# A mixture-of-experts encoder on one core: five token tiles gathered, five multiplied densely, expert blocks summed four at a time

## The chip, the cores and the metric

The kernel runs on one core of a Trainium2 chip. The metric is device time in microseconds, median of the runs; lower is better. One execution was taken by the hardware profiler, and every row below comes from it.

## What is computed

An encoder layer for 1280 tokens (256 of a prompt, 1024 of a sample) of width 1024, in fp32: a mixer (retention and latent attention), cross attention to 256 memory tokens, and a layer of experts, cut here to what matters:

```python
q = (xt @ wq).reshape(128, 8, 256)
s1, s2 = q1 . sub_keys[0], q2 . sub_keys[1]      # 8 heads, 128 keys each
v1, i1 = top_k(s1, 16); v2, i2 = top_k(s2, 16)
ts, sel = top_k(v1[:, None] + v2[None, :], 16)   # ids = i1 * 128 + i2: 16 experts of 16384 per head
g = softmax(ts)
a = einsum('td,ted->te', xt, U[ids])             # 128 experts a token
y = einsum('te,ted->td', g * gelu(a), V[ids])
```

U and V have 16384 rows of 1024 floats. A last RMS norm follows.

## The kernel before, in words

The tokens are ten tiles of 128. After the mixer and cross attention (lines 307 to 870) the experts of a tile are computed in one of two ways, and the list GATHER (line 39) says which.

**Routing** (`lists`, `pairs`, `route`, lines 879 to 992) finds a tile's 128 experts a token with VectorE's top-8 instructions. A tile in GATHER then stores its ids; a dense tile stores the two key numbers and the weight. The last dense tile (KEPT, line 44) hands them over in SBUF instead, and the first dense tile of the last block (HALVED) is routed in two halves.

**Gathered tiles** (`gather`, line 995): for each of 128 expert slots GpSimd issues an indirect DMA that fetches one row of U per token (128 rows of 4 KB, line 1025), and VectorE multiplies it with the tokens and sums (line 1031); 128 slots of V follow, each scaled and added to an accumulator (line 1040). That is 256 row steps a tile. In the pass tokens and accumulator lie in PSUM. Nine row buffers take turns there (line 119 has four, `gather` adds two, and three come at line 147 when the routing is done and its room is given back).

**Dense tiles**: first `gates` (line 1067) makes a table G of every token's weight for every expert from one-hot products, tile by tile, with VectorE, ScalarE, GpSimd and TensorE at work; a step that needs an unrouted tile runs the routing until it is there (line 1082). Then `dense` (line 1147), the **dense pass**, walks the 128 blocks of 128 experts. `a_stage` loads a block of U and V, splits each into a high and a low part (ScalarE copies, GpSimd subtracts: uh, ul, vh, vl), multiplies U with the tokens of both halves of the dense tiles in three matmuls per chunk of 128 (lines 173 to 175), applies Gelu (ScalarE), the gate (VectorE, wr) and splits the result (wh by ScalarE, wl by VectorE). `v_stage` multiplies with V for each tile and sums NG blocks in PSUM before VectorE adds the sum to the tile's accumulator (line 1212). NG is 3: 43 groups. A group's second product is written behind the next group's first one.

**What sets the order of the work.** The program is one Python trace; the tile framework may move instructions by its own view of time, and each engine then runs its own in order. Routing and gathering are generators. After each group of three matmuls `mm3` (line 176) calls `tick` with an estimate of TensorE's time, `tick` (line 123) multiplies it by a share from RHO (line 50; the third pair is the dense pass: first number while tiles are being routed, second while rows alone are left) and `step` (line 136) takes steps from the generators until their own estimates (1.2 for a row, 0.65 to 2.6 for pieces of routing) have used it up. `step` takes routing first and gathering when no routing is left. What is left when the pass has been written comes behind it (line 1268). VectorE's instructions of routing and of rows go through `Fill` (line 80), which ties each behind the last instruction of the main work written before it (`Lead`, line 64): the framework may let it fall later, not draw it ahead of that. For the steps left behind the pass that mark is the pass's start (line 1267).

```python
q = q or self.routing or self.gathering          # line 137
self.slots, self.at = ["grow"] * 4, 0            # line 119
wl = ap.tile([P, H], F32R, tag="wl", ..., bufs=2 * NG + 3)   # line 1185; vh, vl: 2 * NG + 1
```

SyncE's queue issues the loads of U, V and G and the small loads at the start of a gathered tile (ids, weights, tokens, lines 1012 to 1018); GpSimd's queue issues the row fetches, between its subtractions.

## Time and profile before

| | us |
|---|---|
| median of 3 runs | 4372.47 (4365.78 to 4373.7) |
| the profiled execution | 4367.04 |
| its span, first to last instruction | 4365.2 |
| first dense matmul in the profile | 2111.45 |

The engines are PE (TensorE), PEld (its weight loads, which overlap PE), DVE (VectorE), ACT (ScalarE), POOL (GpSimd) and SP (SyncE, DMA issue); a q behind a name is its sequencer. Times are us, and L with a number is a line of the kernel. In a row of the windows each engine has its busy time and instructions; the granted share of TensorE's clock, the mean busy share of 16 DMA engines and what they moved follow. In a row of groups the mean of one instruction is in ns, and behind the second bar stands the engine's idle time just before them with what ended it. Matmuls overlap each other, so the time of one is longer than the distance of two starts. L74 stands for all instructions through `Lead`, L90 for those through `Fill`.

### The profile page before, as it was taken

The page shows a single profiled execution, that of the slowest core. Times are in us where ns is not written, and L with a number is a line of the kernel's source. Part 1 is how long each engine was busy: PE and PEld are TensorE (multiplying, and loading weights), DVE is VectorE, ACT ScalarE, POOL GpSimd, SP SyncE. Part 2 cuts the span into 40 slices and gives each one's busy share as a digit, 9 for nine tenths or more (in the row PEclk, how much of TensorE's full clock was granted, in tenths as well). Part 3 has the DMA queues.
Part 4 walks back from the last instruction along what each step waited for, and adds up shares of the span by engine and source line. Part 5 has one row for each costly group of instructions (what it writes and reads, how often), then busy time and mean ns, then how long its engine had stood idle before and what let it go on. Part 6 is the DMA issues. An engine that isn't in the chain of part 4 may idle for free.

```text
span 4365.2 us, 66436 instructions
## 1 busy us (share of the span) xinstructions
PE 4010.5 (92%) x23202; PEld 3578.9 (82%) x23202; DVE 3281.7 (75%) x7044; ACT 1639.9 (38%) x3569; POOL 2301.6 (53%) x2090
## 2 busy tenths in 40 slices
PE   7999988899788988887798999999999999999999
PEld 7999877666587877876787888888988889888888
DVE  5556422798576799699788878888887888878883
ACT  6333535455343243498522222222222223222223
POOL 2221244013667710277537776666777677766662
PEclk9999999899899989999999999999999999999999
DMA  2112578237789866577648988888888889888882
GB/s 89 37 40 71 202 240 286 80 103 223 261 271 334 278 227 228 186 219 211 212 127 295 325 302 297 311 294 299 310 307 301 285 300 328 316 298 295 289 286 85
DMA packets 489008, 1030.74 MB, mean 236 GB/s; under 512 B 42720, under 2 KB 201952, under 8 KB 488672
## 3 DMA queue, kind: packets, MB, share of 16 engines
q0 software_dynamic: 149536, 545.33, 35.5%
q1 hardware_dynamic: 329200, 470.66, 32.6%
q10 hardware_dynamic: 9936, 10.51, 0.8%
q8 instruction: 182, 2.98, 0.3%
q14 instruction: 154, 1.26, 0.1%
HBM read 901.87 MB, written 124.45 MB: 235 GB/s over the span
## 4 chain that ended last, share of the span: by engine, by line
PE 26%; issue 8%; POOL 6%; DVE 6%; DMA 3%; ACT 1%; SPq 0%; POOLq 0%; ACTq 0%; DVEq 0%
PE pa L175 5%; PE pa L173 5%; PE pa L174 5%; PE pv L174 4%; PE pv L173 4%; PE pv L175 4%; POOL grow L1025 4%; DMA ur<-in_uT 2%; POOL vl L1199 1%; POOL ul L1175 1%; DVE gps L90 1%; DVE wr L74 1%; DVE dacc L74 1%; DVE wl L74 1%; DVE gj L90 1%
## 5 line engine op out<-in xcount | busy, mean ns | idle before, releaser
L1025 POOL DMA_INDIRECT grow<-in_peer_u,gids x512 | 537.1, 1049 | 533.9 <-DVE gj L90 213.0
L1025 POOL DMA_INDIRECT grow<-in_peer_v,gids x512 | 522.5, 1020 | 545.5 <-DVE gps L90 159.9
L173 PE MATMUL pa<-dxT,uh 128*128 128x384 f32 x2048 | 689.0, 337 | 17.4 <-ACT wr L1186 15.0
L174 PE MATMUL pa<-dxT,uh 128*128 128x384 f32 x2048 | 688.6, 336 | 0.0
L175 PE MATMUL pa<-dxT,ul 128*128 128x384 f32 x2048 | 676.4, 337 | 9.3 <-POOL ul L1175 9.3
L173 PE MATMUL pv<-vh,wh 128*128 128x512 f32 x1536 | 603.7, 397 | 40.1 <-DVE dacc L74 40.1
L174 PE MATMUL pv<-vl,wh 128*128 128x512 f32 x1536 | 609.7, 397 | 12.4 <-POOL vl L1199 11.7
L175 PE MATMUL pv<-vh,wl 128*128 128x512 f32 x1536 | 608.9, 396 | 1.4 <-DVE wl L74 1.4
L90 DVE SCALAR_TENSOR_TENSOR gps<-grow,ga,gps 128x1024 f32<-128x1024 f32 x384 | 493.2, 1284 | 9.6 <-ACT gps L1052 2.9
L90 DVE SCALAR_TENSOR_TENSOR gj<-grow,gps 128x1024 bf16<-128x1024 f32 x384 | 466.7, 1215 | 11.2 <-DMA grow<-in_peer_u,gids 3.1
L206 POOL TENSOR_TENSOR wl<-wraw,wh 128x512 fp32r<-128x512 f32 x180 | 250.7, 1409 | 310.7 <-ACT wh L202 241.2
L173 PEld LDWEIGHTS pa<-dxT,uh 128*128 128x128 f32 x2048 | 386.4, 189 | 31.7 <-ACT wr L1186 16.5
L1199 POOL TENSOR_TENSOR vl<-vr,vh 128x512 fp32r<-128x512 f32 x256 | 331.2, 1313 | 146.4 <-ACT vh L1198 144.3
L175 PEld LDWEIGHTS pa<-dxT,ul 128*128 128x128 f32 x2048 | 385.2, 189 | 21.2 <-POOL ul L1175 15.6
L1175 POOL TENSOR_TENSOR ul<-ur,uh 128x512 fp32r<-128x512 f32 x256 | 337.3, 1321 | 106.8 <-ACT uh L1174 103.5
L74 DVE TENSOR_TENSOR dacc<-pv,dacc 128x1024 f32<-128x1024 f32 x258 | 311.8, 1218 | 108.1 <-PE pv L175 107.6
L174 PEld LDWEIGHTS pa<-dxT,uh 128*128 128x128 f32 x2048 | 386.3, 189 | 6.3
L173 PEld LDWEIGHTS pv<-vh,wh 128*128 128x128 f32 x1536 | 292.7, 191 | 104.6 <-DVE dacc L74 48.5
L1174 ACT CAST uh<-ur 128x512 fp32r<-128x512 f32 x256 | 158.3, 621 | 553.4 <-DMA ur<-in_uT 510.2
L74 DVE TENSOR_TENSOR wr<-wr,gt 128x384 f32<-128x384 f32 x256 | 196.2, 767 | 209.2 <-ACT wr L1186 184.2
L174 PEld LDWEIGHTS pv<-vl,wh 128*128 128x128 f32 x1536 | 293.2, 191 | 73.2 <-POOL vl L1199 18.4
L175 PEld LDWEIGHTS pv<-vh,wl 128*128 128x128 f32 x1536 | 292.9, 191 | 58.4 <-DVE wl L74 1.8
(287 smaller groups left out, 9373.8 us busy)
## 6 DMA issues: line engine op xcount, KB each, us to landing
ur<-in_uT SPq DMA_DIRECT2D x256, 256.0 KB, 4.1
vr<-in_peer_v SPq DMA_DIRECT2D x256, 256.0 KB, 4.0
G<-st SPq DMA_DIRECT2D x96, 512.0 KB, 6.2
gt<-G SPq DMA_DIRECT2D x64, 768.0 KB, 7.2
wraw<-in_peer_wq SPq DMA_DIRECT2D x96, 256.0 KB, 5.9
wraw<-in_w_out SPq DMA_DIRECT2D x48, 256.0 KB, 5.1
wraw<-in_ca_wq SPq DMA_DIRECT2D x48, 256.0 KB, 3.6
x<-ld SPq DMA_DIRECT2D x24, 512.0 KB, 6.6
```

Source lines behind the costliest of these rows:

```text
L74: r = f(*a, **kw)
L90: r = f(*a, **kw)
L173: mm(ps, a[0], b[0], start=first, stop=False)
L174: mm(ps, a[0], b[1], start=False, stop=False)
L175: mm(ps, a[1], b[0], start=False, stop=last)
L206: (nc.vector if self.spare and k in self.spare else eng).tensor_tensor(wl[:, :n], raw[:, :n], r32(wh[:, :n]), ALU.subtract)
L1025: nc.gpsimd.indirect_dma_start(out=u, out_offset=None, in_=src, in_offset=bass.IndirectOffsetOnAxis(ap=ids[:, s:s + 1], axis=0))
L1174: nc.scalar.copy(uh, ur)
L1175: nc.gpsimd.tensor_tensor(ul, ur, r32(uh), ALU.subtract)
L1199: nc.gpsimd.tensor_tensor(vl, vr, r32(vh), ALU.subtract)
```

## The change

Tile 7 joins GATHER, so five tiles are gathered and five (2 to 6) are dense; tile 6 is then both HALVED and KEPT. The dense tokens are split into halves of 384 and 256 columns. NG becomes 4, which makes 32 groups and gives W 11 and V 9 buffers. In the dense pass `step` takes gathering and routing in turn, and the share for rows alone is 0.78.

```diff
--- before.py
+++ after.py
@@ -36,7 +36,7 @@
 EPS, GEPS = 1e-6, 1e-5
 NDEC = RH * P + 5 * RH
 
-GATHER = [0, 1, 8, 9]
+GATHER = [0, 1, 7, 8, 9]
 DENSE = [t for t in range(NTILE) if t not in GATHER]
 TD = len(DENSE) * P
 MADE = DENSE
@@ -44,10 +44,10 @@
 HALVED, KEPT = [t for t in MADE if t in BLOCKS[-1]][0], MADE[-1]
 TG = 64
 HP = PK // 2
-NG = 3
+NG = 4
 O1_BY = "va"
 
-RHO = ((0.75, 0.7), (0.5, 0.0), (0.9, 0.55))
+RHO = ((0.75, 0.7), (0.5, 0.0), (0.9, 0.78))
 LATE = 2
 
 MORE = 3
@@ -117,6 +117,7 @@
         self.owed, self.rho = 0.0, (0.0, 0.0)
         self.gps = self.rp = None
         self.slots, self.at = ["grow"] * 4, 0
+        self.turn = 0
         self.anchor = None
         self.v, self.vf = Lead(self), Fill(self)
 
@@ -134,7 +135,12 @@
             self.owed -= self.step()
 
     def step(self, q=None):
-        q = q or self.routing or self.gathering
+        if q is None:
+            q = self.routing or self.gathering
+            if self.rho is RHO[2] and self.gathering:
+
+                self.turn += 1
+                q = (self.gathering if self.turn % 2 else self.routing) or q
         try:
             return next(q[0])
         except StopIteration:
@@ -1149,7 +1155,9 @@
         dx, xT = self.dx, self.xT
         v = self.v
         nd = len(DENSE)
-        H = TD // 2
+
+        H = nd // 2 * P + nd % 2 * P
+        halves = [(0, H), (H, TD)]
         NTG = TD // TG
         vb = I["peer_v"].rearrange("(b i) d -> b i d", b=PK)
         with ExitStack() as es:
@@ -1176,7 +1184,8 @@
                         U.append((uh, ul))
                     Wb = []
                     for hf in range(2):
-                        hs = slice(hf * H, (hf + 1) * H)
+                        c0, c1 = halves[hf]
+                        hs, H = slice(c0, c1), c1 - c0
                         ps = pa.tile([P, 512], F32, tag="pa", name=self.nm("pa"))
                         for k in range(KC):
                             self.mm3(ps[:, :H], [u[:, k % 4, :] for u in U[k // 4]], (xT[0][:, k, hs], xT[1][:, k, hs]), k == 0, k == KC - 1)
@@ -1185,7 +1194,7 @@
                         wl = ap.tile([P, H], F32R, tag="wl", name=self.nm("wl"), bufs=2 * NG + 3)
                         nc.scalar.activation(wr, ps[:, :H], AF.Gelu)
                         w3 = wr.rearrange("p (g t) -> p g t", t=TG)
-                        v.tensor_tensor(w3, w3, self.gt[:, hf * NTG // 2:(hf + 1) * NTG // 2, n % 2, :], ALU.mult)
+                        v.tensor_tensor(w3, w3, self.gt[:, c0 // TG:c1 // TG, n % 2, :], ALU.mult)
                         nc.scalar.copy(wh, wr)
                         v.tensor_tensor(wl, wr, r32(wh), ALU.subtract)
                         Wb.append((wh, wl))
@@ -1204,7 +1213,7 @@
 
             def v_stage(W, V):
                 for n in range(nd):
-                    hf, at = divmod(n * P, H)
+                    hf, at = divmod(n * P, halves[0][1])
                     ps = pv.tile([P, D], F32, tag="pv", name=self.nm("pv"))
                     for j in range(len(W)):
                         for c in range(2):
```

## Rows read from the trace of the kernel before

**Rows 1.** The page, part 1: busy us, share of the span, instructions.
```profile
PE 4010.5 (92%) x23202; PEld 3578.9 (82%) x23202; DVE 3281.7 (75%) x7044; ACT 1639.9 (38%) x3569; POOL 2301.6 (53%) x2090
```

**Rows 2.** Windows of the dense pass: length; PE, PEld, DVE, ACT, POOL; clock, DMA, GB/s.
```profile
2111.00:2272.00 161.00, 139.02 (x694) 125.27 (x693) 126.44 (x505) 49.48 (x85) 56.41 (x41) 0.96 0.50 159
2272.00:4256.00 1984.00, 1925.34 (x9566) 1734.55 (x9565) 1644.55 (x1899) 515.08 (x939) 1397.39 (x1262) 0.99 0.85 301
4256.00:4365.20 109.20, 101.16 (x502) 90.44 (x500) 42.94 (x53) 35.38 (x63) 24.14 (x19) 0.98 0.25 85
```

**Rows 3.** Waits, 2300 to 4250 us: total us, times, longest us.
```profile
POOL grow L1025 <- DVE gps L90: 180.6, 123, 10.3
...
DVE wr L74 <- ACT wr L1186: 157.9, 73, 6.6
...
PE pv L173 <- DVE dacc L74: 31.7, 13, 4.1
...
PE pv L174 <- POOL vl L1199: 11.7, 8, 3.7
```

**Rows 4.** Timeline of TensorE in the pass, 384 columns: start us, us.
```profile
2111.71 0.34 PE L174 MATMUL pa<-dxT,uh 128*128 128x384 f32 x1
...
2117.95 0.33 PE L174 MATMUL pa<-dxT,uh 128*128 128x384 f32 x1
```

**Rows 5.** Timeline of TensorE, first projections, 256 columns.
```profile
149.79 0.28 PE L175 MATMUL pj<-wh,xl 128*128 128x256 f32 x1
...
154.07 0.28 PE L175 MATMUL pj<-wh,xl 128*128 128x256 f32 x1
```

**Rows 6.** Timeline of TensorE in the pass, second product, 512 columns.
```profile
3310.08 0.39 PE L174 MATMUL pv<-vl,wh 128*128 128x512 f32 x1
...
3316.88 0.39 PE L174 MATMUL pv<-vl,wh 128*128 128x512 f32 x1
```

**Rows 7.** Windows, tile grow alone (row buffers): DVE, ACT, POOL busy; clock, DMA, GB/s.
```profile
2272.00:4256.00 1984.00, 1036.69 (x1202) 7.02 (x12) 810.56 (x808) 0.99 0.85 301
```

**Rows 8.** Groups by line, 2111 to 4366 us: busy, mean ns, idle before.
```profile
L1175 POOL TENSOR_TENSOR ul<-ur,uh 128x512 fp32r<-128x512 f32 x253 | 333.5, 1321 | 106.8 <-ACT uh L1174 103.5
L1199 POOL TENSOR_TENSOR vl<-vr,vh 128x512 fp32r<-128x512 f32 x256 | 331.2, 1313 | 146.4 <-ACT vh L1198 144.3
L74 DVE TENSOR_TENSOR dacc<-pv,dacc 128x1024 f32<-128x1024 f32 x258 | 311.8, 1218 | 108.1 <-PE pv L175 107.6
...
L74 DVE TENSOR_TENSOR wl<-wr,wh 128x384 fp32r<-128x384 f32 x256 | 231.8, 906 | 66.5 <-ACT wh L1189 64.4 <-PE pv L175 1.6
L74 DVE TENSOR_TENSOR wr<-wr,gt 128x384 f32<-128x384 f32 x256 | 196.2, 767 | 209.2 <-ACT wr L1186 184.2 <-ACT root L186 21.1 <-DMA vr<-in_peer_v 3.5
```

**Rows 9.** Timeline of GpSimd and VectorE, 3338 to 3390 us.
```profile
3338.52 0.94 POOL L1025 DMA_INDIRECT grow<-in_peer_v,gids  x1 [0.30 <-issue]
3339.77 0.94 POOL L1025 DMA_INDIRECT grow<-in_peer_v,gids  x1 [0.31 <-issue]
...
3364.02 5.03 POOL L1199 TENSOR_TENSOR vl<-vr,vh 128x512 fp32r<-128x512 f32 x4
...
3365.41 4.05 DVE L74 TENSOR_TENSOR wl<-wr,wh 128x384 fp32r<-128x384 f32 x1
...
3389.01 0.55 DVE L74 TENSOR_TENSOR wl<-wr,wh 128x384 fp32r<-128x384 f32 x1
```

**Rows 10.** A window of 20 us in the pass, columns as in rows 2.
```profile
3040.00:3060.00 20.00, 20.00 (x99) 17.64 (x98) 15.86 (x25) 4.84 (x9) 16.75 (x16) 1.00 1.02 402
```

**Rows 11.** Waits of SyncE's DMA queue, 2300 to 4250 us.
```profile
SPq L1014 <- DVE ga L90: 14.7, 1, 14.7
```

**Rows 12.** Windows of the gate making, 1827 to 2111 us, summed; timeline of TensorE there.
```profile
sum 284.00, PE 222.50 PEld 196.57 DVE 275.65 ACT 261.49 POOL 216.79; mean PE 55.62 PEld 49.14 DVE 68.91 ACT 65.37 POOL 54.20
...
2065.56 0.42 PE L1093 MATMUL ps<-c_ident,g 128*128 128x128 f32 x1
...
2111.45 0.42 PE L173 MATMUL pa<-dxT,uh 128*128 128x384 f32 x1
```

## The prediction

> **What bounds the kernel now.** I read the page's busy times first: TensorE is busy 92% of the span, VectorE 75%, GpSimd 53% [rows 1]. A mean over stages says little, so next come the windows. From 2111 us to the end (2254 us) runs the dense pass, and in its main stretch of 1984 us TensorE is busy 1925 us at a granted clock of 0.99, VectorE 1645, GpSimd 1397, the DMA engines 0.85 [rows 2]. The waits say which way the engines lean on each other [rows 3]: VectorE waits for ScalarE's Gelu (157.9 us), which waits for TensorE; GpSimd waits for VectorE to give a row buffer back (180.6 us); TensorE waits for an eviction 31.7 us in all. So TensorE bounds the pass, and the rows of the gathered tiles ride along. The pitch of its matmuls, first start against last, is 0.1733 us at 384 columns (36 in 6.24 us [rows 4]), 0.1189 at 256 (36 in 4.28 us [rows 5]) and 0.2267 at 512 (30 in 6.80 us [rows 6]). 6144 x 0.1733 + 4608 x 0.2267 = 2109 us of the 2254.
>
> **Sum made against** the profiled execution, 4367 us (span 4365.2), 5 us under the median of 4372.5.
>
> **TensorE.** Five dense tiles: the first product has 3072 matmuls of 384 and 3072 of 256 columns, 532 + 365 us; the second has 3840 of 512, 871 us. Together 1768 us, 341 less than now. Weight loads need no term of their own: the 0.1189 was measured with one load per matmul. Where TensorE waits more, its clock may fall; at the 0.96 of the pass's first stretch [rows 2] the same work takes 1842 us, still less than what follows.
>
> **VectorE.** In the pass it is busy 126 + 1645 + 43 = 1814 us [rows 2]. One more gathered tile is 256 rows; all work on row buffers took 1036.69 us for 808 rows [rows 7], 1.283 us each with the start and finish of a tile in it: +328. Evictions fall from 43 groups x 6 tiles = 258 to 32 x 5 = 160, at 1.218 us [rows 8]: -119. The gate product and the residue (wr, wl) keep their 512 instructions; a half of them get a third narrower, and of the 0.55 us that one takes undisturbed [rows 9] I let a third go: 256 x 0.18 = -46. Routing of tile 7 moves into the pass. It has no clean row: the 126 us that VectorE was busy in the first 161 us of the pass hold two tiles' routing, wr, wl and evictions, so one tile is under 63 us; 30 would leave over half of the stretch to the others. I take 45, nearer the middle, and keep 30 and 63 as ends. Sum 1814 + 328 - 119 - 46 + 45 = **2022 us**, more than TensorE's 1768. VectorE becomes the longer one.
>
> The mean wr and wl (0.767 and 0.906 us [rows 8]) lie well over 0.55, and one row shows why: a wl of 4.05 us starts inside a GpSimd run of four vl subtractions of 5.03 us and ends with it [rows 9]. I keep the excess of 256 x (0.22 + 0.36) = 148 us as it is; if each further GpSimd instruction held VectorE as much, it would grow with GpSimd's work below (a fifth), by 30 us, and that is the other end. The Trainium skill, SBUF — State Buffer, section "Who interferes with whom", says that a VectorE instruction with two SBUF inputs contends with a GpSimd one that reads SBUF, and not with one that only writes. By that rule the ul and vl subtractions count, whose number does not change; the sum would be the 2022 us, against 2052 by the other end.
>
> **GpSimd.** A row's descriptors take 810.56/808 = 1.003 us [rows 7], and from one to the next 1.25 us pass where nothing is waited for (3338.52 to 3339.77 [rows 9]). Now 812 of them stand in the pass (44 rows are left of tile 0, and three tiles), after the change 1068. With 512 subtractions at 1.32 us [rows 8] the queue needs 812 x 1.25 + 676 = 1691 us now, and 1068 x 1.25 + 676 = **2011 us** after. That is level with VectorE, and in order: a descriptor that waits for a row buffer holds the ul and vl behind it, for which TensorE waits.
>
> **DMA.** 159 x 161 + 301 x 1984 + 85 x 109 = 632 MB in the pass [rows 2]; 256 rows of 0.524 MB make 766. The best 20 us moved 402 GB/s at a share of 1.02 [rows 10]; at that rate 1905 us. SP gets four loads and a store more, for one more tile's start and end; the ids load at a tile's start held SP 14.7 us [rows 11], with weight loads queued behind it. I cost that at nothing, since four raw buffers stand ahead; without that cover it is 15 us. ScalarE is busy 600 us of the pass [rows 2] and gets copies of under 10 us more: nothing.
>
> **Where the rows stand.** The planner credits the gathering 0.78 of its own estimate of TensorE's time (line 50) and charges 1.2 for a row (lines 1032, 1041). Its estimate for the pass is 128 x 12.8 = 1638. While three tiles are routed in turn with rows (35.4 units each, 0.9 credited) 245 pass with 95 rows; the other 1393 x 0.78 / 1.2 give 906. So 1001 of 1068 rows stand in the pass, and **67 behind it**, where they may be drawn forward only behind the row before them. Before, the same count ends at 1851 of 1966, which is the idle end in the last 109 us of rows 2. Nine row buffers are there as before, but three of them only when routing is done, now about 15% into the pass.
>
> **The pass after.** VectorE's 2022, plus its waits. wl on ScalarE's copy, 66.5 us [rows 8], stays: it is a latency. The waits for TensorE, 157.9 at wr [rows 3] and 108.1 at the eviction [rows 8], shrink as TensorE gets ahead; none left would be 0, all left 266. I keep a quarter, 66 us, nearer to none, since TensorE has 1768 us of work against 2022. Start and end idled 35 + 66 us [rows 2]; rows now begin with the pass and fill its end, and I keep 30. 2022 + 66 + 66 + 30 = 2184 us, **70 less** than 2254.
>
> **Ahead of the pass.** Gate making for six tiles runs from 1827 us to the first dense matmul at 2111.45; VectorE is busy 275.65 of 284 us and ScalarE 261.49 [rows 12]. The sixth tile (7) got its last transpose at 2065.56, so its own piece is 46 us, and at least that goes. A sixth of the stage and 45 us of routing, 92, go at most. ScalarE then binds: 261.49 x 5/6 = 218, and I add some 10 for its first transposes: 228, **56 less**.
>
> Sum: 4367 - 56 - 70 = 4241.
>
> **Rivals.**
> A, the three queues dovetail: the waits for TensorE vanish and the pass ends with VectorE's 2022 and 38 us: 4117. For it: in gate making VectorE is busy 275.65 of 284 us [rows 12], 0.97, beside a ScalarE as full. Against: GpSimd's 2011.
> B, the DMA engines bind. At the main stretch's 301 GB/s for 0.85 [rows 2] full is 354: 766 MB take 2164 us, and with 70 us of thin start and end 2234: 4291. Against: the 402 of rows 10. The Trainium skill, DMA: Bandwidth & Descriptors, section "Where 436 GB/s comes from", gives about 358 GB/s as the limit between HBM and SBUF; by it 2140 us, and the sum would be 4267. The 20 us at 402 do not agree with it as a ceiling.
> C, slower: a convoy. GpSimd stands at a descriptor until VectorE frees a row buffer, the vl behind it are late, TensorE is late, and VectorE waits at wr in its own order. Then VectorE's share stays what it is, 1814/2254 = 0.805, and 2022/0.805 = 2512 us give 4569. It decides under 2022/2310 = 0.875. For it: the 180.6 us in which GpSimd stands at such descriptors, and 11.7 us of TensorE waiting for vl [rows 3]; with four blocks a group holds eight vl where it held six, and only one vl can be made ahead of a group, as now. Against: nearly all of VectorE's other idle time now is waiting for TensorE, which will be ahead.
> D, it does not do what it says: the scheduler places instructions by its own view of time, and if the pass holds no more rows than at 0.55, 95 + 1393 x 0.55/1.2 = 733, then 335 stand behind it at 1.283: 430 us after 1768 and TensorE's idle 144: 2342 us, 4399.
>
> **How the numbers follow.** Forecast 0.56, A 0.15, B 0.11, C 0.13, D 0.05. The predicted time is 4241. The range goes down to A (4117) and up past B and the forecast's bad ends (266 - 66 of waits, 30 of contention, 18 of routing: 4489 together, 4365 for half of it) to 4370; it leaves out C, D and half of A. Under 0.2% (9 us) a measurement of this kernel cannot tell from no change. Faster 0.80 (forecast, A, most of B), same 0.06, slower 0.14.
>
> **What would show it.** Right: first dense matmul near 2055 us; 256 rows more and 98 evictions fewer in the pass; VectorE at 0.92 or more and TensorE near 0.82 of the pass; GpSimd's subtractions and descriptors nearly back to back; about 67 rows after the last second product. Wrong: TensorE still above 0.93 (A), DMA share at 0.97 with rows late (B), VectorE under 0.88 with long waits of TensorE for vl (C), hundreds of rows at the end (D).

## The result, and the profile after

The changed kernel takes 4395.3 us (median of 6 runs, 4389.4 to 4405.4), the kernel before 4370.9 on the same chip: a ratio of 1.0061, with a 95% interval of 1.0048 to 1.0074. It is slower by 0.6%; 4241 was forecast, with 0.14 for slower. The profiled execution has a span of 4391.6 us against 4365.2, 26 more: gate making and what lies ahead of it give back 64 (the first dense matmul starts at 2047.3 instead of 2111.45 [rows 12]), and from there to the end it is 2344 us instead of 2254, 90 more where 70 less were forecast.

The page, part 1 (busy us, share of the span, instructions), which answers to [rows 1]:

```profile
PE 3715.7 (85%) x22175; PEld 3280.2 (75%) x22175; DVE 3393.2 (77%) x7220; ACT 1548.1 (35%) x3465; POOL 2488.2 (57%) x2314
```

The windows of the pass (length; PE, PEld, DVE, ACT, POOL busy; clock, DMA share, GB/s), cut where its routing ends and where the last second product ends; they answer to [rows 2]:

```profile
2047.30:2470.00 422.70, 370.90 (x1983) 330.24 (x1982) 385.38 (x1001) 122.78 (x229) 241.40 (x201) 0.94 0.73 239
2470.00:4219.40 1749.40, 1547.85 (x8006) 1360.36 (x8004) 1460.49 (x1873) 428.56 (x863) 1348.83 (x1262) 0.95 0.94 341
4219.40:4391.60 172.20, 0.00 (x0) 0.00 (x0) 162.69 (x130) 2.85 (x6) 108.52 (x115) 0.51 0.94 366
```

And the same windows for the tile grow alone (row buffers: DVE, ACT, POOL busy; clock, DMA share, GB/s), as in [rows 7]:

```profile
2047.30:2470.00 422.70, 140.36 (x151) 1.17 (x2) 107.47 (x101) 0.94 0.73 239
2470.00:4219.40 1749.40, 1072.81 (x1318) 8.22 (x14) 821.86 (x853) 0.95 0.94 341
4219.40:4391.60 172.20, 159.19 (x124) 0.00 (x0) 108.52 (x115) 0.51 0.94 366
```

VectorE is busy 385 + 1460 + 163 = 2009 us of the pass, almost the 2022 of the sum, and rows cost what they cost before. What is wrong is the share, 2009/2344 = 0.857. The row descriptors, counted in these windows, come at 1749/853 = 2.05 us in the main stretch, and the last 115 are issued when TensorE has nothing left to do.

The longest waits of VectorE and GpSimd in the whole pass, and of TensorE up to its last second product (total us, times, longest us), against [rows 3]:

```profile
DVE wr L74 <- ACT wr L1195: 209.7, 116, 10.3
DVE dacc L74 <- PE pv L181: 48.1, 50, 3.0
...
POOL grow L1031 <- DVE gps L90: 146.9, 235, 6.7
POOL grow L1031 <- DVE gj L90: 130.8, 190, 5.0
...
PE pa L181 <- POOL ul L1183: 65.0, 29, 5.8
PE pv L180 <- POOL vl L1208: 63.3, 41, 3.6
PE pv L179 <- ACT wh L1198: 46.0, 36, 10.4
```

In the kernel before, the row for ul from 2300 to 4250 us, which stands beside the one for vl in [rows 3], is:

```profile
PE pa L175 <- POOL ul L1175: 7.3, 10, 1.5
```

TensorE used to wait 11.7 us for vl and 7.3 for ul in nearly the whole pass and now waits 63 and 65. The two make 128 of the 253 us that it is idle up to its last second product; it is busy 371 + 1548 = 1919 us. VectorE's waits for it, which the forecast cut to a quarter of 266, are 210 + 48 = 258. The three engines stand in a ring: GpSimd at a descriptor until VectorE gives a row buffer back, TensorE for the ul and vl behind that descriptor, VectorE (wr, dacc) for TensorE. The timeline shows one turn of it, first GpSimd's queue (start us, us, then the instruction, idle before and what ended it), then TensorE:

```profile
2868.27 0.95 POOL L1031 DMA_INDIRECT grow<-in_peer_u,gids  x1 [1.48 <-DVE gps L90]
2871.49 0.94 POOL L1031 DMA_INDIRECT grow<-in_peer_u,gids  x1 [2.27 <-DVE gps L90]
2874.62 0.94 POOL L1031 DMA_INDIRECT grow<-in_peer_u,gids  x1 [2.19 <-DVE gps L90]
...
2877.10 1.27 POOL L1183 TENSOR_TENSOR ul<-ur,uh 128x512 fp32r<-128x512 f32 x1
...
2878.43 0.45 PE L181 MATMUL pa<-dxT,ul 128*128 128x384 f32 x1 [1.52 <-POOL ul L1183]
```

GpSimd is idle for 1.48, 2.27 and 2.19 us until VectorE gives row buffers back, and the ul behind them comes 1.52 us too late. In many other waits no descriptor ahead of the low part stands, as here in GpSimd's queue:

```profile
3085.35 0.95 POOL L1031 DMA_INDIRECT grow<-in_peer_u,gids  x1 [0.16 <-DVE gj L90]
3086.61 0.94 POOL L1031 DMA_INDIRECT grow<-in_peer_u,gids  x1 [0.30 <-DVE gj L90]
3087.85 0.94 POOL L1031 DMA_INDIRECT grow<-in_peer_u,gids  x1 [0.30 <-DVE gj L90]
3088.81 1.30 POOL L1208 TENSOR_TENSOR vl<-vr,vh 128x512 fp32r<-128x512 f32 x1
...
3094.48 0.94 POOL L1031 DMA_INDIRECT grow<-in_peer_u,gids  x1 [0.30 <-DVE gj L90]
3095.44 1.27 POOL L1208 TENSOR_TENSOR vl<-vr,vh 128x512 fp32r<-128x512 f32 x1
```

and TensorE at the same time:

```profile
3096.77 0.50 PE L180 MATMUL pv<-vl,wh 128*128 128x512 f32 x1 [2.91 <-POOL vl L1208]
...
3100.41 0.45 PE L181 MATMUL pa<-dxT,ul 128*128 128x384 f32 x1 [1.86 <-POOL ul L1183]
```

Three or four descriptors, about 1.25 us from one to the next, then one subtraction, then descriptors again; TensorE takes up each low part as soon as it is there, and has stood for it. The 0.16 and 0.30 us before these descriptors are no standing: as much passes in [rows 9] where nothing is waited for, though the profile names a releaser for many of them. This second picture is the usual one. If the trace's waits of TensorE for ul and vl from 2470 us on, 127 us, are laid over GpSimd's queue, GpSimd is at subtractions for 68 of them, at descriptors and their issue for 55, and stands at a descriptor for under 2. At the moment when TensorE waits, GpSimd is at work; standing can make a low part late only from earlier on, by leaving more work in front of it.

The groups by line of the whole execution (busy us, mean ns | idle before), against [rows 8]:

```profile
L74 DVE TENSOR_TENSOR dacc<-pv,dacc 128x1024 f32<-128x1024 f32 x160 | 193.8, 1218 | 48.5 <-PE pv L181 48.1
...
L74 DVE TENSOR_TENSOR wr<-wr,gt 128x384 f32<-128x384 f32 (+1 forms) x256 | 175.6, 689 | 231.4 <-ACT wr L1195 209.7 <-ACT root L192 21.6
...
L74 DVE TENSOR_TENSOR wl<-wr,wh 128x384 fp32r<-128x384 f32 (+1 forms) x256 | 171.2, 676 | 9.6 <-ACT wh L1198 9.3
```

### The profile page after: what moved, and what is told of

Same layout as the page of the kernel before. It is cut to its first block, busy times and chain, and to the rows that moved or that the text cites. A ratio compares the mean times of both kernels' runs of the same rounds, so it can differ in the third digit from the quotient of the medians.

```text
span 4391.6 us, 65244 instructions
## 1 busy us (share of the span) xinstructions
PE 3715.7 (85%) x22175; PEld 3280.2 (75%) x22175; DVE 3393.2 (77%) x7220; ACT 1548.1 (35%) x3465; POOL 2488.2 (57%) x2314
## 4 chain that ended last, share of the span: by engine, by line
PE 26%; DVE 20%; issue 14%; POOL 12%; DMA 4%; ACT 4%; SPq 1%; POOLq 0%; ACTq 0%; DVEq 0%
POOL grow L1031 8%; DVE gps L90 4%; PE pa L181 3%; PE pa L179 3%; PE pa L180 3%; PE pv L181 2%; PE pv L180 2%; DVE gj L90 2%; PE pv L179 2%; POOL vl L1208 2%; POOL ul L1183 2%; PE pj L179 2%; PE pj L181 2%; PE pj L180 2%; DVE o L74 1%
## 5 line engine op out<-in xcount | busy, mean ns | idle before, releaser
L1031 POOL DMA_INDIRECT grow<-in_peer_u,gids x640 | 649.3, 1015 | 583.6 <-DVE gj L90 195.4
L1031 POOL DMA_INDIRECT grow<-in_peer_v,gids x640 | 635.7, 993 | 528.1 <-DVE rs L90 154.2
L181 PE MATMUL pa<-dxT,ul 128*128 128x384 f32 (+1 forms) x2048 | 631.8, 321 | 65.3 <-POOL ul L1183 65.0
L179 PE MATMUL pa<-dxT,uh 128*128 128x384 f32 (+1 forms) x2048 | 654.7, 320 | 16.1 <-ACT wr L1195 11.6
L90 DVE SCALAR_TENSOR_TENSOR gps<-grow,ga,gps 128x1024 f32<-128x1024 f32 x512 | 658.8, 1287 | 12.1
L180 PE MATMUL pa<-dxT,uh 128*128 128x384 f32 (+1 forms) x2048 | 646.7, 319 | 0.0
L90 DVE SCALAR_TENSOR_TENSOR gj<-grow,gps 128x1024 bf16<-128x1024 f32 x512 | 622.1, 1215 | 17.0 <-DMA grow<-in_peer_u,gids 3.8
L1195 ACT ACTIVATE wr<-pa 128x384 f32<-128x384 f32 (+1 forms) x256 | 111.2, 437 | 983.4 <-PE pa L181 970.0
L74 DVE TENSOR_TENSOR wr<-wr,gt 128x384 f32<-128x384 f32 (+1 forms) x256 | 175.6, 689 | 231.4 <-ACT wr L1195 209.7
L179 PE MATMUL pj<-act,wh 128*128 128x256 f32 x1088 | 313.3, 297 | 11.2 <-ACT wh L208 5.4
L181 PE MATMUL pj<-act,wl 128*128 128x256 f32 x1088 | 307.0, 293 | 9.4 <-POOL wl L212 8.5
```

The source lines that it names most:

```text
L74: r = f(*a, **kw)
L90: r = f(*a, **kw)
L179: mm(ps, a[0], b[0], start=first, stop=False)
L180: mm(ps, a[0], b[1], start=False, stop=False)
L181: mm(ps, a[1], b[0], start=False, stop=last)
L1031: nc.gpsimd.indirect_dma_start(out=u, out_offset=None, in_=src, in_offset=bass.IndirectOffsetOnAxis(ap=ids[:, s:s + 1], axis=0))
```

## The experiments

Each run against the kernel before on its chip; the changed kernel is at 1.0061, with 4219 and 122 in the last two columns. "End of TensorE" is the end of the last second product in the trace, "rows behind" counts VectorE's instructions on rows after it. A difference in us below is taken from 4395.3 and so between chips, on which the kernel before took 4370.5 to 4375.0: some 5 us of it carry no meaning. The rows behind differ as well, so a part of each difference can lie in where the rows stand. Letters name theories; each expectation says what its letters stand for.

| run | us | ratio (95%) | end of TensorE | rows behind |
|---|---|---|---|---|
| e1_no_sub | 4159.2 | 0.9504 (0.9477 to 0.9531) | 3949 | 150 |
| e2_half_dma | 4275.7 | 0.9770 (0.9742 to 0.9798) | 4075 | 139 |
| e2b_half_dve | 4387.3 | 1.0029 (1.0017 to 1.0041) | 4256 | 88 |
| e3_no_turn | 4416.5 | 1.0090 (1.0068 to 1.0112) | 4203 | 151 |
| e4_rho95 | 4402.9 | 1.0063 (1.0042 to 1.0084) | 4232 | 122 |
| e5_ng3 | 4395.5 | 1.0046 (1.0031 to 1.0062) | 4197 | 139 |
| e6_ng3_rows12 | 4446.6 | 1.0162 (1.0138 to 1.0186) | 4317 | 87 |
| e7_share_v1 | 4381.3 | 1.0016 (1.0003 to 1.0029) | 4176 | 140 |
| e8_free_sub | 4311.7 | 0.9866 (0.9843 to 0.9889) | 4123 | 132 |
| e9_low_last | 4372.7 | 1.0010 (1.0000 to 1.0020) | 4237 | 92 |
| e10_low_last_share | 4352.8 | 0.9964 (0.9945 to 0.9983) | 4214 | 96 |
| e11_before_low_last | 4375.3 | 1.0010 (0.9996 to 1.0024) | | |
| e13_half_order | 4392.2 | 1.0048 (1.0033 to 1.0063) | 4264 | 94 |
| e14_half_order_half_share | 4353.8 | 0.9955 (0.9942 to 0.9969) | 4207 | 95 |
| e15_half_order_share3 | 4348.5 | 0.9945 (0.9924 to 0.9966) | 4200 | 100 |
| e16_second_low_last_v | 4388.9 | 1.0041 (1.0030 to 1.0051) | 4249 | 94 |
| e17_second_low_last_uv | 4385.9 | 1.0036 (1.0023 to 1.0048) | 4247 | 95 |
| e18_all_cover | 4359.9 | 0.9977 (0.9967 to 0.9986) | 4182 | 128 |

**Which engine.** Three kernels take load off one engine each. e1_no_sub leaves out GpSimd's subtractions:

```diff
-                        nc.gpsimd.tensor_tensor(ul, ur, r32(uh), ALU.subtract)
-                        U.append((uh, ul))
+                        U.append((uh, uh))
...
-                        nc.gpsimd.tensor_tensor(vl, vr, r32(vh), ALU.subtract)
-                        Vb.append((vh, vl))
+                        Vb.append((vh, vh))
```

> The changed kernel without GpSimd's 512 subtractions of the dense pass (ul and vl; the high part stands in the low part's place, so the products lose their residue terms' meaning but not their matmuls). Theory G, GpSimd's queue in order: its work in the pass falls from about 2011 to 1336 us, the 127 us that TensorE waits for ul and vl go, and with them VectorE's waits for ScalarE's Gelu; 100 to 200 us less, 4200 to 4295. Theory D, the DMA engines at a share of 0.94: no byte less moves, at most the last 6% of the main stretch's 1749 us can be had, and what it gains is under 60 us: 4335 to 4390. Theory V, VectorE's own 2009 us: as G.

e2_half_dma fetches half rows, and VectorE reads `u[:, :D // 2]` twice over:

```diff
-            nc.gpsimd.indirect_dma_start(out=u, out_offset=None, in_=src,
+            nc.gpsimd.indirect_dma_start(out=u[:, :D // 2] if banked else u, out_offset=None, in_=src.rearrange("n (a b) -> (n a) b", a=2) if banked else src,
```

> The changed kernel with half of each row fetched in the dense pass (512 of 1024 columns, which VectorE reads twice): 1068 rows of 0.262 MB, 280 MB less of about 740; VectorE's elements, GpSimd's descriptors and TensorE's work stay. Theory D: the DMA share falls to about 0.6 and the pass ends 150 us or more earlier, 4240 or less. Theory G: the ul and vl are as late as before, TensorE waits for them as long (100 us or more), and the time changes by under 40 us, 4350 to 4400. Theory V: under 40 us too.

e2b_half_dve works on half of each row (`D2` is 512 in the pass), in both products of a gathered tile:

```diff
-            v.scalar_tensor_tensor(junk, u, 1.0, x3, ALU.mult, ALU.mult, accum_out=a[:, s:s + 1])
+            v.scalar_tensor_tensor(junk[:, :D2], u[:, :D2], 1.0, x3[:, :D2], ALU.mult, ALU.mult, accum_out=a[:, s:s + 1])
...
-            v.scalar_tensor_tensor(acc, u, a[:, s:s + 1], acc, ALU.mult, ALU.add)
+            v.scalar_tensor_tensor(acc[:, :D2], u[:, :D2], a[:, s:s + 1], acc[:, :D2], ALU.mult, ALU.add)
```

> The changed kernel with VectorE's work on each row cut to 512 of 1024 columns; the whole row is fetched. VectorE's 2009 us of the pass fall by 1068 x 0.6 = 640. Theory V: 250 us or more less, 4140 or less. Theory G: descriptors and subtractions, 2011 us, stay; the first 423 us give some 60 and the tail of 122 rows at the descriptor's pitch of 1.25 instead of 1.33 some 10, so 4300 to 4385, and TensorE still waits 100 us or more for ul and vl. Theory D: as G, at a share of 0.95 or more.

The same 860 us of the main stretch, 2470 to 3330 us, in four kernels, each with the columns of the windows above. First the changed kernel, whole and for grow alone:

```profile
2470.00:3330.00 860.00, 759.37 (x3958) 670.40 (x3957) 719.60 (x909) 208.18 (x421) 674.10 (x634) 0.96 0.95 347
...
2470.00:3330.00 860.00, 538.96 (x634) 3.52 (x6) 412.33 (x430) 0.96 0.95 347
```

e1_no_sub:

```profile
2470.00:3330.00 860.00, 822.81 (x4489) 737.29 (x4488) 743.61 (x965) 236.76 (x481) 434.18 (x457) 0.99 0.99 378
```

e2_half_dma, whole and for grow alone:

```profile
2470.00:3330.00 860.00, 814.16 (x4372) 717.31 (x4371) 803.79 (x966) 233.99 (x459) 727.95 (x673) 0.98 0.74 231
...
2470.00:3330.00 860.00, 564.26 (x655) 3.51 (x6) 439.60 (x450) 0.98 0.74 231
```

e2b_half_dve:

```profile
2470.00:3330.00 860.00, 752.90 (x3880) 663.65 (x3879) 487.57 (x868) 203.31 (x412) 654.26 (x619) 0.94 0.93 341
```

VectorE falls to 488 of 860 us in e2b_half_dve, and TensorE gets no further for it (3880 matmuls against 3958). Its time goes into waiting: for wr, 543.9 us up to the last second product, where it was 197.5. Half of its row work gives 8 us (14 by the ratios): VectorE's own work does not bind, and theory V falls. Without the subtractions TensorE gets 13% more done in the same time, and the kernel is 236 us faster, more than theory G named; theory D, which allowed 60, falls as a bound, since the DMA engines carry 378 GB/s there, 31 more than in the changed kernel. But half the bytes give 120 us, under D's 150 and well over G's 40. In e2_half_dma GpSimd's queue is full: 450 descriptors at 1.25 us and 288 us of subtractions are 851 of 860 us. In the changed kernel the same account is 430 x 1.25 + 262 = 800, and in the other 60 GpSimd is idle. The waits from 2470 us to the last second product show what the half rows did, e2_half_dma:

```profile
PE pv L180 <- POOL vl L1214: 5.9, 9, 1.4
PE pa L181 <- POOL ul L1189: 4.5, 7, 1.5
...
POOL grow L1031 <- DVE gj L90: 37.8, 102, 3.2
POOL grow L1031 <- DVE gps L90: 17.2, 48, 3.6
...
DVE wr L74 <- ACT wr L1201: 39.2, 41, 2.9
```

GpSimd is fuller than before and yet ul and vl are on time (10 us of waits instead of 127); its waits for row buffers are 55 us instead of 221. Such rows count the 0.16 to 0.31 us before a descriptor too; what its idle time before descriptors has beyond 0.31 us each is 29 us instead of 152. So a full queue alone need not make ul and vl late. The run changes more than one thing, and does not separate them: a row lands 3.8 us after its issue instead of 6.2 to 6.3 (medians, 2470 to 4000 us), and a load of U or V after 3.0 to 3.1 instead of 5.0. That rows which land earlier give their buffers back earlier is argued here, not shown; against the loads as the cause speaks that GpSimd waits only 25 us of the changed kernel's main stretch for ScalarE's copies of them.

**The parts of the change.** e3_no_turn takes the turn out of step():

```diff
-            if self.rho is RHO[2] and self.gathering:
-                self.turn += 1
-                q = (self.gathering if self.turn % 2 else self.routing) or q
```

> The changed kernel with step() as before it: the pass's routing goes first, rows start when all of it is placed. By the planner 80 rows stay behind the pass instead of 67. Theory T, that routing in turn with rows costs (the first 423 us hold 101 rows with six buffers, VectorE full): nine buffers are there from about 2250 and the rows run at 25 in 50 us from then on; 50 to 100 us less, 4300 to 4345. Theory G or D alone (the rows' pace in the main stretch is what counts): the time changes by under 25 us, 4370 to 4420.

e4_rho95 raises the planner's share of the pass:

```diff
-RHO = ((0.75, 0.7), (0.5, 0.0), (0.9, 0.78))
+RHO = ((0.75, 0.7), (0.5, 0.0), (0.9, 0.95))
```

> The changed kernel with the gathering's share at 0.95 instead of 0.78 (RHO[2][1]). The planner's count then runs out of rows inside the pass: 95 + 1393 x 0.95/1.2 = 1198 of 1068 wanted. Theory Tail (the 172 us behind the last second product, in which TensorE does nothing, are what the change loses): the tail falls to about 40 us and the pass grows little; 100 us less than the changed kernel's 4395, 4270 to 4320. Theory G (GpSimd's queue paces the pass): each of the 122 rows costs the pass 1.25 us of the same queue and more waits of TensorE; tail and pass exchange about evenly, 4360 to 4440.

e5_ng3 and e6_ng3_rows12 change sizes:

```diff
-NG = 4
+NG = 3
```

> The changed kernel with three blocks in a group instead of four: 215 evictions instead of 160, 55 x 1.22 = 67 us more on VectorE; rows, descriptors and subtractions as they are. Theory V (VectorE's work counts): 40 to 70 us more, 4435 to 4465. Theory G: they fit beside, within 25 us of 4395.

```diff
-NG = 4
-MORE = 3
+NG = 3
+MORE = 6
```

> As e5_ng3, with twelve row buffers instead of nine once routing is done (the room of the fourth block). Theory L (GpSimd stands 221 us of the main stretch at descriptors whose row buffer is not free yet, because rows land late at a DMA share of 0.94): three more buffers take most of that standing away, 80 to 180 us less than e5_ng3. Theory G in its plain form (the instructions on GpSimd are what counts): the standing goes to other places, within 30 us of e5_ng3.

Theory T falls: without the turn the kernel is not faster, but 21 us slower. By the ratios, which compare each kernel with the one before on its own chip, it is 13, and their intervals overlap, so that the turn pays is not shown. Groups of four instead of three are worth nothing: 67 us of VectorE's work more, and the time is the same. The share of 0.95 moves no row out of the tail: behind the last second product stand the same 172.2 us, with the same counts as in the changed kernel (columns as in the windows above; e4_rho95):

```profile
4232.10:4404.30 172.20, 0.01 (x1) 0.00 (x0) 162.76 (x130) 2.85 (x6) 108.59 (x115) 0.51 0.94 366
```

So raising the planner's share does not take the 122 rows away from there, and what the tail is worth by itself this run cannot say. Twelve row buffers, which by theory L would end the standing, cost 51 us against e5_ng3: from 2470 us to the last second product GpSimd waits for row buffers 274 us (e5_ng3: 202), and TensorE waits 163 us for vl instead of 86. That more descriptors are let ahead of a vl, and the ring only becomes longer, is argued.

**Load or lateness.** One kernel moves a quarter of the load, one keeps the load and cuts TensorE loose from it.

```diff
-                        nc.gpsimd.tensor_tensor(vl, vr, r32(vh), ALU.subtract)
+                        (v if c in (1,) else nc.gpsimd).tensor_tensor(vl, vr, r32(vh), ALU.subtract)
```

> The changed kernel with one of a block's four subtractions (the second vl, 128 of 512) on VectorE instead of GpSimd: GpSimd gives up 128 x 1.30 = 167 us, VectorE takes on 128 x about 0.65 = 83. Theory G: TensorE's waits for ul and vl fall from 127 us to under 60 and the time by 60 to 130 us, 4265 to 4335. Theory V: 40 us or more slower than 4395.

e8_free_sub still computes ul and vl, and gives TensorE the high parts:

```diff
-                        U.append((uh, ul))
+                        U.append((uh, uh))
...
-                        Vb.append((vh, vl))
+                        Vb.append((vh, vh))
```

> The changed kernel with GpSimd's 512 subtractions kept, but no matmul reads what they write (the high part stands in the low part's place, as in e1_no_sub). GpSimd's queue is as full as in the changed kernel, its row descriptors and buffers as late; only TensorE no longer waits for it, but for ScalarE's copies alone. In the order of the program 132 rows follow the last eviction, 122 in the changed kernel. Theory C (coupling: it is the lateness of ul and vl behind descriptors that costs, through TensorE's clock and VectorE's waits too): most of e1_no_sub's 236 us, 4160 to 4260. Theory G (the load on GpSimd's queue itself): under 60 us less than 4395, 4335 to 4400.

e7 gives 14 us, outside theory G's 60 to 130: TensorE now waits 64.5 us for the vl on VectorE, whose queue is in order and full of rows too. e8 gives 83 us, between the two theories. The waits from 2470 us to the last second product, e8_free_sub:

```profile
POOL grow L1031 <- DVE gj L90: 53.3, 122, 5.1
POOL grow L1031 <- DVE gps L90: 36.5, 75, 4.2
...
DVE wr L74 <- ACT wr L1195: 83.3, 69, 6.9
```

With TensorE free, VectorE's wait for wr falls from 197.5 to 83 us, and with it GpSimd's waits for row buffers from 221 to 90 (152 to 54 beyond the 0.31 us), though the instructions of neither engine were changed. That is the ring, opened at one place. GpSimd's queue then has 697 us busy with 437 descriptors in the 860 us, which at 1.25 us each and with the subtractions fill 819; the 153 us from e8 to e1 come when its load goes as well, and with the load the time by which the subtractions stretch VectorE's wr and wl (see Contention below). These two are not told apart.

**Cover for the low parts.** The products that read ul and vl are put last in each accumulation; then subtractions are moved as well.

In the first product (the second has the same form, with vh read by wh and wl of all blocks before vl):

```diff
-                        for k in range(KC):
-                            self.mm3(ps[:, :H], [u[:, k % 4, :] for u in U[k // 4]], (xT[0][:, k, hs], xT[1][:, k, hs]), k == 0, k == KC - 1)
+                        for k in range(KC):
+                            for i in range(2):
+                                nc.tensor.matmul(ps[:, :H], U[k // 4][0][:, k % 4, :], xT[i][:, k, hs], start=k + i == 0, stop=False)
...
+                        for k in range(KC):
+                            nc.tensor.matmul(ps[:, :H], U[k // 4][1][:, k % 4, :], xT[0][:, k, hs], start=False, stop=k == KC - 1)
...
```

> The changed kernel with the products that need a low part of a weight put last in each accumulation: 16 matmuls of a first product read uh before 8 read ul, 16 (of four blocks) of each half of a second product read vh before the 8 that read vl. The same matmuls. TensorE gets 2 to 4 us of cover for ul and vl, whose waits are 2.2 and 1.7 us each (65 us in 29, 60 in 35). In the order of the program 92 rows follow the last eviction instead of 122. Theory C: most of the 127 us of waits go, 60 to 130 us less than 4395, 4265 to 4335. Theory G: GpSimd's 2011 us of instructions stay, and the waits come back behind the cover; under 30 us, 4365 to 4400.

e10_low_last_share adds e7_share_v1's line; e11_before_low_last makes e9's edit in the kernel before.

> e9_low_last with e7_share_v1's edit as well (the second vl of a block on VectorE). Theory C: e7 exchanged a wait for GpSimd by one for VectorE's queue, and with the cover both are hidden; 20 to 60 us less than e9_low_last. Theory G: it is worth what it was worth alone, 14 us, within 25 us of e9_low_last.

> The kernel before the change with e9_low_last's order of the products. There TensorE waits 19 us for ul and vl in the main stretch, and its work fills 0.97 of it. Theory C: at most those, 10 to 25 us less than 4371. If the order has a price of its own (another order of the weight loads, second halves waiting for each other), it shows here as 0 or more.

e9 gives 23 us, as theory G had it: the waits for vl are gone, those for ul are 138 us instead of 65. e10, 20 less again, fits both theories. In the kernel before the order changes nothing: there TensorE waits little for low parts, and its own work binds.

e13_half_order, where the ul of four tiles follow the uh of the same four (`low` is 0, then 1):

```diff
-                        for k in range(KC):
-                            self.mm3(ps[:, :H], [u[:, k % 4, :] for u in U[k // 4]], (xT[0][:, k, hs], xT[1][:, k, hs]), k == 0, k == KC - 1)
+                        for c in range(0, KC, 4):
+                            for low in range(2):
+                                for k in range(c, c + 4):
+                                    for i in range(2 - low):
+                                        nc.tensor.matmul(ps[:, :H], U[c // 4][low][:, k - c, :], xT[i][:, k, hs], start=k + i + low == 0,
...
```

> As e9_low_last for the second product; in the first product the ul matmuls follow the uh matmuls of the same half of four tiles (8, then 4) instead of all sixteen. Theory C with the buffer as e9's cost: e9 held both halves' uh and ul to the end of the product, and with three buffers the next ul came later; here the waits for ul fall from 135 us to the 65 or less of the changed kernel, and the time to 4320 to 4360. Theory G: the lateness is GpSimd's load and finds another place; within 15 us of e9_low_last's 4373.

e14_half_order_half_share, on top of it (`self.rp is None` once routing is done):

```diff
-                        nc.gpsimd.tensor_tensor(ul, ur, r32(uh), ALU.subtract)
+                        (v if self.rp is None and c in (4,) else nc.gpsimd).tensor_tensor(ul, ur, r32(uh), ALU.subtract)
...
-                        nc.gpsimd.tensor_tensor(vl, vr, r32(vh), ALU.subtract)
+                        (v if self.rp is None and c in (1,) else nc.gpsimd).tensor_tensor(vl, vr, r32(vh), ALU.subtract)
```

> e13_half_order with two of a block's four subtractions (the second ul and the second vl) on VectorE, once routing is done. GpSimd gives up about 206 x 1.30 = 268 us, VectorE takes on 206 x 0.65 = 134 and loses up to 206 x 0.16 = 33 of stretched wr and wl. Theory G: GpSimd's queue is the bound of the main stretch, and the time falls by 60 to 130 us against e13. Theory V from here on: VectorE, 0.835 busy there, fills up to over 0.95 and its own lateness holds TensorE; within 30 us of e13.

e15_half_order_share3 has `c in (0, 4)` for ul.

> e14_half_order_half_share with the first ul on VectorE as well (three of four). GpSimd's load is then 400 us below the changed kernel's, VectorE's 200 us above. Theory G: GpSimd is no longer the bound; no more than 20 us better than e14. Theory V: 20 to 80 us slower than e14.

e13 is a miss: 4392, with 129 us of waits for ul, so a buffer held longer is not what limited e9, and why e9 is 20 us better stays open. On top of it e14 gives 38 us, between theory G's 60 and theory V's 30, and e15 5 more, as theory G had it. In e15_half_order_share3 the same 860 us read:

```profile
2470.00:3330.00 860.00, 772.62 (x4020) 685.52 (x4019) 818.15 (x1075) 211.10 (x424) 509.40 (x490) 0.95 0.95 352
```

VectorE is busy 0.95 of it now, and GpSimd 0.59: the load has changed sides, and VectorE is nearly full. Of the versions that compute what the reference does this has the lowest median: 0.9945 of the kernel before, 47 us under the changed kernel. Its interval overlaps those of e14 and e10, so these runs do not say which of the three is the fastest.

The next two kernels ask which operand is late. In e16 the first product is as in the changed kernel, the second has its low products last, and both vl stand on VectorE:

```diff
-                        nc.gpsimd.tensor_tensor(vl, vr, r32(vh), ALU.subtract)
+                        (v if self.rp is None and c in (0, 1) else nc.gpsimd).tensor_tensor(vl, vr, r32(vh), ALU.subtract)
```

> The changed kernel with the low products last in the second product only (the first as in the changed kernel), and both vl of a block on VectorE once routing is done; both ul stay on GpSimd. Load as in e14 (a half of the subtractions moved). Theory C (the operand without cover must not stand in a queue with rows, but GpSimd, with half its subtractions gone, has it on time): waits for ul under 40 us and 20 to 60 us less than e14's 4354. Theory V (the load of VectorE decides): within 20 us of e14, 4335 to 4375.

The second, e17_second_low_last_uv, has the second ul on VectorE too.

> e16 with the second ul on VectorE too, three quarters moved as in e15. Theory V: within 15 us of e15's 4349. Theory C: the ul on VectorE is late as in e14 and e15, so 20 us or more slower than e16.

e16 takes 4388.9 us and e17 4385.9, both outside every range named. The waits of e16 from 2470 us to the last second product tell most:

```profile
PE pa L181 <- POOL ul L1183: 169.9, 53, 7.7
...
POOL grow L1031 <- DVE gj L90: 247.3, 316, 4.5
POOL grow L1031 <- DVE gps L90: 239.9, 290, 7.3
```

GpSimd has half its subtractions gone, and ul comes later than ever: 170 us of waits. The load that left the queue is replaced by standing: 487 us of waits for row buffers, and 335 us of idle time before descriptors beyond 0.31 us, where the changed kernel has 152. Beside e2_half_dma, where a full queue has ul on time, this says that standing makes a low part late even where the load is small. How much it does so in each kernel can be estimated from the trace: if every descriptor is moved forward by the time that it stood beyond 0.31 us, a subtraction still waits for its copy, and nothing else moves, 25 of e16's 170 us of waits are left, but 69 of the changed kernel's 127. In the changed kernel, then, some half of the lateness is standing, and the other half is work queued ahead of the low part.

e18_all_cover has e9's order in both products and e14's two subtractions on VectorE, and:

```diff
-NG = 4
+NG = 3
...
-                        uh = dx.tile([P, 4, P], F32R, tag="uh", name=self.nm("uh"), bufs=3)
-                        ul = dx.tile([P, 4, P], F32R, tag="ul", name=self.nm("ul"), bufs=3)
+                        uh = dx.tile([P, 4, P], F32R, tag="uh", name=self.nm("uh"), bufs=4)
+                        ul = dx.tile([P, 4, P], F32R, tag="ul", name=self.nm("ul"), bufs=4)
```

> e9_low_last's order in both products, four buffers of uh and ul instead of three (their room comes from groups of three blocks, which e5 showed to cost nothing), and the second ul and the second vl of a block on VectorE once routing is done, as in e14. In the order of the program 128 rows follow the last eviction, 95 in e14. Theory C (lateness of ul and vl is what is left): waits for ul and vl under 40 us in all, 4290 to 4335. Theory V (VectorE, at 0.95 of the main stretch with e15's share, is the bound; 55 evictions more, 67 us, come on top): 4345 to 4400.

Here TensorE waits for ul 27.9 + 9.4 us and not for vl, as theory C has it, and the time is theory V's: 4359.9. VectorE is busy 816 of the same 860 us, and the longest wait of TensorE, 67 us, is for wh, which ScalarE copies from VectorE's wr. That what is left is VectorE's queue is read from this; no run takes load off VectorE in this order.

## Why the prediction was wrong

**Right.** Gate making: 64 us less, 56 forecast; the stage from 1826 us to the first dense matmul, as in [rows 12], is 221 us long where 228 were worked out, and ScalarE fills it:

```profile
1826.00:2047.30 221.30, 174.70 (x1295) 156.47 (x1296) 202.56 (x668) 215.41 (x568) 182.56 (x164) 0.97 0.72 207
```

The work of the engines: VectorE 2009 us for 2022. GpSimd has 1069 descriptors at 1.25 and 1698.75 - 1037.85 = 661 us of subtractions, 1997 for 2011. Evictions are 160 at 1.218 us, as counted. (The wait in [rows 11] that the forecast gives to the load of the ids is that of the weights beside it, line 1014; nothing hangs on it.)

**The step that failed** is the term for VectorE's waits in "The pass after": "I keep a quarter, 66 us, nearer to none, since TensorE has 1768 us of work against 2022". It measured 258. The wait of wl on ScalarE's copy, kept at 66.5, went to 9.6, and the rest of the idle time is 46 for 30. 2009 + 258 + 9.6 + 22 (wr's wait for root) + 46 is the 2344. The reason given does not hold either: TensorE needs 2172 us to its last second product, 1919 busy and 253 idle, and only then come the 172 us of the tail, with 122 rows. By the same count of matmuls 1768 were worked out; it is some 50 short of the busy time in the kernel before too (2165 for 2109) and in e1_no_sub (1820 for 1768). TensorE did not get ahead, since what it reads is made in the queue that was filled most: GpSimd has work for 0.91 of the main stretch, VectorE for 0.83. The forecast had GpSimd "level with VectorE" at 2011 us and then let the pass follow VectorE alone; e2b_half_dve shows that half of VectorE's row work gives 8 us. Of GpSimd's 2344 us in the pass 347 are idle: 422.7 - 126 - 134 = 163 while routing lasts, 156 in the main stretch, 28 in the tail. Cutting TensorE loose from the low parts gives back 83 us (e8_free_sub), and leaving out their subtractions as well 236 (e1_no_sub), more than the 154 by which the forecast missed. TensorE's granted clock took part: 0.95 to 0.96 in the main stretch where it was 0.99 [rows 2], and 0.99 again in e1_no_sub, where TensorE does not stand for low parts and is busy 1820 us with the same matmuls instead of 1919.

**The rivals.** C came in part, and at a smaller size. Its mechanism is the ring: e8 shows the link from TensorE to VectorE and GpSimd, and e16 the one from standing to late low parts, which in the changed kernel is about half of their lateness by the estimate above. Its sign was a share of VectorE under 0.875, and it is 0.857. Its price kept the old share of 0.805 (4569), which was too much. What it had for it, 180.6 us in which GpSimd stood at descriptors [rows 3], was the first link of that ring; that it stayed hidden because TensorE was the longest is argued. With a chance of 0.13 it was taken too lightly. B does not hold: main stretch and e1 differ in what they move, 341 and 378 GB/s, so 354 is no ceiling, though half the bytes help. The Trainium skill, DMA: Bandwidth & Descriptors, section "Where 436 GB/s comes from", gives about 358 GB/s for a core's share of HBM; e1_no_sub moves 378 over 860 us at a share of 0.99 and does not agree with it as a limit of one core alone. D came in part: 122 rows stand behind the pass for 67 planned, and a higher share (e4_rho95) moves none of them. That its 4399 lies next to the measured 4395 is luck: it has 335 rows behind a TensorE that ends after 1912 us, where there are 122 behind one that ends after 2172. A did not come.

**The first stretch** holds about the 101 rows that were planned (95), but takes 423 us, TensorE being busy 371 of them, where the planner's count had 245 us of TensorE's work: VectorE is 0.91 busy there with routing, and six row buffers serve. The forecast's sums for VectorE and GpSimd were right, and their speed there was never priced. e3_no_turn shows that routing ahead of the rows is no better.

**Contention.** wr and wl take 689 and 676 ns, and 487 each without GpSimd's subtractions (e1_no_sub, groups by line):

```profile
L74 DVE TENSOR_TENSOR wr<-wr,gt 128x384 f32<-128x384 f32 (+1 forms) x256 | 124.2, 487 | 144.7 <-ACT wr L1193 122.6 <-DMA gt<-G 21.5
L74 DVE TENSOR_TENSOR wl<-wr,wh 128x384 fp32r<-128x384 f32 (+1 forms) x256 | 123.3, 487 | 15.4 <-ACT wh L1196 15.4
```

The subtractions thus cost VectorE 256 x (0.202 + 0.189) = 100 us of the pass, and the descriptors, which e1 keeps, next to nothing: at 384 columns wr and wl take 556 ns there, as one does undisturbed in [rows 9]. The Trainium skill, SBUF — State Buffer, section "Who interferes with whom", says that VectorE's instructions with two SBUF inputs contend with GpSimd's reads of SBUF; the trace agrees with it.

**Open.** What the tail of 122 rows is worth alone: e4 was meant to put those rows into the pass and moved none. How the 153 us between e8 and e1 divide into GpSimd's load and the contention. Why e9's order is 20 us better than e13's. Whether GpSimd's order could be written so that no descriptor stands ahead of a ul whose buffer is not free; that was not tried either.

## What to carry to other kernels

When work is added to an engine that is not the longest, look at what else stands in its queue: if the longest engine takes operands from there, in order behind instructions that wait for a third engine, sums of busy time do not settle the end, and the waits between the three must be followed around the ring. Before forecasting that a wait will shrink because its engine gets ahead, check what that engine itself will wait for. Look then at what the engine in front does while the others wait: here it was at work in nearly all of that time, and more row buffers made the kernel slower (e6). And a relief that moves work to another in-order queue with the same rows in it can move the wait along: here the load alone gave 14 us (e7), cover alone 23 (e9), and both together 43 (e10).

## What was not expected of the hardware

DMA moved 378 GB/s over 860 us at a share of 0.99 (e1_no_sub), where the changed kernel has 347 at 0.95 in the same stretch. A subtraction of 512 columns, 1.30 us on GpSimd, takes 0.81 us (ul) and 0.93 us (vl) on VectorE in e15_half_order_share3. And three row buffers more made the kernel 51 us slower.
